# Seven-product pairs of a hybrid decoder layer: three products accumulated on the first one's bank, and a new order of the products

## The chip, the cores and the metric

One Trainium2 chip, one of its cores. The metric is device time in microseconds (us) of one execution, the median of several runs. Engines: PE (TensorE, matmuls) with its weight loads (PEld), DVE (VectorE), ACT (ScalarE), POOL (GpSimd) and SP (SyncE, which issues transfers). PSUM, into which PE writes, has eight banks here, of 128 partitions x 512 fp32 each.

## What is computed

One layer over 1024 tokens of width 1024, in fp32:

```python
h = rms_norm(x, norm_mix_pre[l])
proj = h @ w_in[l]
q, k, v, cb, cc, cx, g_att, g_conv = jnp.split(proj, IN_SPLITS, axis=-1)
...
m   = sigmoid(g_att) * y_att + sigmoid(g_conv) * y_conv
x   = x + RMSNorm_post(m @ W_out)
h   = RMSNorm_pre_ffn(x)
[a, g] = causal_dwconv3(h @ W_up)
x   = x + RMSNorm_post_ffn((gelu(g) * a) @ W_down)
```

y_att is a stick-breaking attention of 8 heads, y_conv a gated short convolution. The change touches the products of h with parts of W_in (the convolution's inputs and the gates) and of h with W_up (1024 x 5632).

## The kernel before

**Numbers and products.** Each fp32 operand of a matmul is held as two fp16 halves, a high and a low one, and a product is three passes (high by high, high by low, low by high) that accumulate in PSUM. Weight tiles of 128 columns are taken two at a time as a pair. A pair's 2 x 2 block product over two halves of the tokens is made with seven block products instead of eight (a Strassen-like scheme): sums and differences of the weight blocks (s_u, ws_u on DVE; their halves wh_u on ACT and DVE) and of the token blocks (hT, hB, tp, tb, n) go in, and the seven results are added up to the pair's two outputs, ca and cg, each with a low (lo) and a high (hi) half of 512 tokens. One product is 12 matmuls of 128 x 512 with start set on the first of those that begin a bank.

The pairs are x0 and x1 (begun in an earlier stage), b0, b1 and g1 to g7 of the mixer (`pair_open`, `pair_prod`), and u0 to u21 of the up-projection (`up_open`, `up_prod`). A pair has three PSUM banks, a, b and c. Before, bank a takes products 1 and 2, one behind the other; bank b takes 6, 7 and 4; bank c takes 5 and 3. Each is a group of its own, so each must be emptied before the next one starts in its bank: 1, 5 and 2 by a copy on ACT (L1413, L1417, L1419 for u), 6, 7, 4 and 3 by an addition on DVE (L1410), and 7 has a second DVE addition of product 5's copy (L1422). PE runs 1, the previous pair's 4, 6, 5, 2, 7, 3. For g pairs the results also go through a sigmoid on ACT.

**Order of the work.** A planner (class Plan) takes all operations with their estimated costs and due times and writes out each engine's instruction list; each engine then runs its list strictly as written and waits on semaphores. Operations marked seq, the products among them, keep the order of the code on PE. Banks come from a ring of eight, five of pool pz (banks 3 to 7) and three of pool pm (banks 0 to 2); a tile gets a bank when its first operation is written out:

```python
self.order, self.n = [p for p, k in pools for _ in range(k)], 0
p = self.order[self.n % len(self.order)]
```

A matmul that starts in a bank waits until the last reader of the tile that had the bank before is done.

**The start of the up-projection.** While the last token tiles are still being normalised and transposed, a few products are run ahead, in this order (pair, product):

```python
PRE = ((0, 1), (1, 1), (0, 2), (1, 2), (2, 1), (2, 2), (0, 5))
```

Names in that stretch: x is the mixer's output with its residual, hn the normalised tile, pt_0 and pt_1 the PSUM tiles with the two halves of tile 7's transposes (L1296), hb their copies (ACT, L1336), tp_0 and tp_1 PSUM tiles with sums of token blocks of tile 6 that DVE makes, n the fp16 halves of those (ACT L1249 the high, DVE L1250 the low), hB and hT the transposed operands that transfers and copies fill from n, hb and tb. jk_u (L66) is a pass over the next weights for their scale, pr_u a tiny matmul for the same purpose, ws_u the weights as they are loaded (SP), wh_u_0 the halves that u2's products 1 and 2 read.

**Later.** Each u pair's ca and cg go through convolution taps (ACT L1434, DVE L1436, twice each), gelu (L1446) and a product (L1447), and the result through the down-projection (pq, pd), with sums kept in DRAM by POOL transfers.

Of the kernel before, what the change touches and what calls it, by code (L numbers as in the profile page):

```python
# [47 lines left out]
class Layer:  # L48
# [693 lines left out]
    def rest(self):  # L742
# [231 lines left out]
        def pair_open(n, p):  # L974
            p.name, p.old = n, begun.get(n)
            p.ca, p.cg = [Buf("x", lambda c=c: self.xp.tile([P, T], F32, tag="x", name=f"{c}{n}")) for c in ("ca", "cg")]
            p.ug = p.ca if p.old else slab(f"ug{n}", [P, T])
            p.bank = {b: Buf("pm", lambda b=b: self.bank(f"p{n}{b}")) for b in ("bc" if p.old else "abc")}
            if p.old:
                p.c = given("s", p.old.c)  # L980
            if n[0] == "g":
                p.sc = Buf("sm", lambda: self.small(f"sc_{n}"))
                V(0.12, lambda: self.mul(p.sc.t[:, 0:1], inv_h, p.sb.t["inv"]), [p.sb], [p.sc])

        def pair_prod(p, i):
            wt, wc = PARTS[i]
            b, ca, cg, ug = p.bank[{1: "a", 2: "a", 5: "c", 3: "c"}.get(i, "b")], p.ca, p.cg, p.ug
            first, gate = i in (1, 6, 5), p.name[0] == "g"

# [12 lines left out]
            p1, pr = ((lambda: p.c.t[:, 0]), (p.c, "0")) if p.old else ((lambda: cg.t[:, lo]), (cg, "l"))  # L1002
            if i == 1:
# [16 lines left out]
            if gate and i in (3, 7, 4):  # L1020
                o, oc, og = {3: (ca, hi, "h"), 7: (cg, hi, "h"), 4: (cg, lo, "l")}[i]
                sigm(o, oc, og, lambda: o.t[:, oc], (o, og))

        def conv_taps(p, i):
# [91 lines left out]
        for n, name in enumerate(PAIRS):  # L1116
            p, kind, i = pw[name], name[0], int(name[1])
            need(n + 2)
            pair_open(name, p)
            start, *middle = (5, 6, 3, 7) if p.old else (1, 6, 5, 2, 7, 3)  # L1120
            pair_prod(p, start)
            if n:
                pair_prod(pw[PAIRS[n - 1]], 4)
                last = PAIRS[n - 1]
                if last[0] == "g":
                    d = int(last[1])
                    sig["gc", d], sig["ga", d] = pw[last].ca, pw[last].cg
                    if d > 1:
                        merge(d)
                else:  # L1130
                    (conv_taps if last[0] == "x" else conv_gate)(pw[last], int(last[1]))
            if name == "g1":
                s_m = p_split()
            for x in middle:
                pair_prod(p, x)
                if name == "x0" and x == 7:
                    wa_branch(6, range(2))
                    wa_branch(7, range(2))
                if name == "g2" and x == 6:
                    wc_branch(0)  # L1140
                    wc_branch(1)
                    merge(0)
                    merge(1)
            if kind == "g":
                if i == 3:
                    wo_sb = wo_sums()
                if i == 5:
                    dn_sums()
                if i == 7:
                    wo = wo_load()  # L1150
                if i == 7:
# [241 lines left out]
        def up_prod(f, i):  # L1393
            p = up[f]
            wt, wc = PARTS[i]
            b = p.bank[{1: "a", 2: "a", 5: "c", 3: "c"}.get(i, "b")]
            ca, cg, ug = p.ca, p.cg, p.ug
            first = i in (1, 6, 5)

            def mm():  # L1400
                n = 0
# [7 lines left out]
            def vadd(o, oc, og, x, xr):  # L1409
                V(C["Vp"], lambda: vec.tensor_tensor(o.t[:, oc], b.t, x.t[:, xr[0]], ALU.add),  # L1410
                  [b, (x, xr[1])], [(o, og)])
            if i == 1:
                A(C["Ah"], lambda: act.activation(cg.t[:, lo], b.t, AF.Copy), [b], [(cg, "l")])  # L1413
            elif i == 6:
                vadd(ca, hi, "h", cg, (lo, "l"))
            elif i == 5:
                A(C["Ah"], lambda: act.activation(ug.t[:, lo], b.t, AF.Copy), [b], [(ug, "l")])  # L1417
            elif i == 2:
                A(C["Ah"], lambda: act.activation(ca.t[:, lo], b.t, AF.Copy), [b], [(ca, "l")])  # L1419
            elif i == 7:  # L1420
                vadd(cg, hi, "h", cg, (lo, "l"))
                V(C["Vh"], lambda: vec.tensor_tensor(cg.t[:, hi], cg.t[:, hi], ug.t[:, lo], ALU.add), [(ug, "l")], [(cg, "h")])  # L1422
# [289 lines left out]
        with tc.manual_schedule(engines={ET.PE, ET.DVE, ET.Activation, ET.SP, ET.Pool}):  # L1712
# [25 lines left out]
            def steps():  # L1738
                for f in range(NFF):
# [228 lines left out]
```

## Time and profile before

| what | value |
|---|---|
| median of 3 runs | 1250.31 us (1249.78 to 1251.18) |
| the profiled execution | 1250.17 us, span of its instructions 1248.5 us |
| mean granted PE clock | 0.998 |
| busy PE / PEld | 1232.6 us (99%) / 559.0 us (45%) |
| busy DVE / ACT / POOL | 1051.7 us (84%) / 841.9 us (67%) / 86.3 us (7%) |

The span runs from the first to the last instruction; 1.67 us of the execution's time lie outside it. Busy PE is counted from modelled ends, so a product of 12 matmuls shows as 2.75 us although the next one starts 2.59 us after it. In rows of the timeline, a square bracket gives the idle time of the engine ahead of the row and who ended it; x12 is the count of instructions in the row.

### The profile page before, as it was taken

What the parts mean: (1) busy time and instruction counts of PE and PEld (TensorE: products, weight loads), DVE (VectorE), ACT (ScalarE), POOL (GpSimd) and SP (SyncE); (2) the same over time, 40 slices, a digit from 0 to 9 for tenths busy, and PEclk for the clock granted to TensorE, in tenths of its full rate; (3) what the DMA queues carried; (4) which work ended last, traced back from release to release, by engine and by line L of the source; (5) the groups of instructions that cost most, each with busy time, mean ns of one, the idle gap of its engine ahead of it and who ended that gap; (6) DMA issues with size and microseconds to landing.
All of it is one profiled execution on the core that took longest, in us unless ns stands there. A gap on an engine that the chain in (4) does not pass through costs nothing.

```text
span 1248.5 us, 16492 instructions
## 1 busy us (share of the span) xinstructions
PE 1232.6 (99%) x6065; PEld 559.0 (45%) x6065; DVE 1051.7 (84%) x1661; ACT 841.9 (67%) x1219; POOL 86.3 (7%) x113
## 2 busy tenths in 40 slices
PE   9999999999999999999999999999999999999997
PEld 4444444444444444444444444444444444444443
DVE  7988889856999776569899999799799879979976
ACT  7766666736758465665676669778777967878424
POOL 1100000000000000001100001002100300211003
PEclk9999999999999999999999999999999999999999
DMA  8755677661214121657853205415921961594608
GB/s 280 158 134 107 141 131 178 146 147 34 69 68 135 35 68 51 220 186 169 218 144 135 68 11 218 177 34 101 261 77 19 193 194 34 99 255 150 170 3 133
DMA packets 148932, 160.81 MB, mean 129 GB/s; under 512 B 114425, under 2 KB 114553, under 8 KB 148850
## 3 DMA queue, kind: packets, MB, share of 16 engines
q1 hardware_dynamic: 138480, 123.05, 35.3%
q0 software_dynamic: 10368, 36.70, 14.2%
q8 instruction: 47, 0.77, 0.2%
q14 instruction: 35, 0.29, 0.1%
q10 hardware_dynamic: 2, 0.00, 0.0%
HBM read 92.88 MB, written 37.75 MB: 105 GB/s over the span
## 4 chain that ended last, share of the span: by engine, by line
PE 45%; DVE 2%; DMA 2%; ACT 1%; issue 1%; POOL 1%; POOLq 0%; DVEq 0%; ACTq 0%
PE pq L1563 12%; PE pd L1633 2%; PE pd L1666 1%; DMA ws_u<-w_up_nt 1%; PE pu7b L1404 1%; PE pu20b L1404 1%; PE pu17b L1404 1%; PE pu15b L1404 1%; PE pu13b L1404 1%; PE pu10b L1404 1%; PE pu9b L1404 1%; PE pu6b L1404 1%; PE pu4b L1404 1%; PE pu2b L1404 1%; PE pu21b L1404 1%
## 5 line engine op out<-in xcount | busy, mean ns | idle before, releaser
L1404 PEld LDWEIGHTS <-wh_u 128*128 128x128 f16 x1848 | 179.2, 98 | 218.6 <-issue 2.0
L992 PEld LDWEIGHTS <-wh_g 128*128 128x128 f16 x588 | 57.1, 98 | 68.6
L827 DVE SCALAR_TENSOR_TENSOR wh_u<-ws_u,sc_u,wh_u 128x1024 f16<-128x1024 f32 (+1 forms) x66 | 72.2, 1103 | 13.9 <-ACT wh_u L825 13.4
L1208 PE MATMUL py<-wo,m 128*128 128x512 f16 x384 | 83.3, 379 | 0.0
L825 ACT ACTIVATE wh_u<-ws_u,sc_u 128x1024 f16<-128x1024 f32 (+1 forms) x66 | 66.4, 1008 | 23.6 <-PE pu0c L1404 4.2
L1567 ACT ACTIVATE st<-pq,sd 128x512 f32<-128x512 f32 x112 | 73.9, 699 | 9.9 <-DVE ua L1447 5.6
L791 POOL DMA_DIRECT2D acc<-st x56 | 43.8, 783 | 426.8 <-ACT st L1567 426.8
L66 ACT ACTIVATE jk_u<-ws_u 128x1024 bf16<-128x1024 f32 x44 | 46.4, 1054 | 23.6 <-DMA ws_u<-w_up_nt 23.2
L624 DVE TENSOR_TENSOR_SCAN e<-e,mask 128x512 f32<-128x512 f32 (+3 forms) x64 | 48.6, 806 | 13.3 <-ACT e L617 13.3
L1208 PEld LDWEIGHTS <-m 128*128 128x128 f16 x384 | 37.4, 98 | 44.9
L1436 DVE SCALAR_TENSOR_TENSOR ua<-ca,cw_a,ua 128x1023 f32<-128x1023 f32 (+1 forms) x44 | 56.2, 1278 | 1.0 <-ACT ua L1434 0.9
L1436 DVE SCALAR_TENSOR_TENSOR ug<-cg,cw_g,ug 128x1023 f32<-128x1023 f32 (+1 forms) x44 | 56.2, 1277 | 0.1
L617 ACT ACTIVATE e<-z,cz 128x1024 f32<-128x1024 f32 (+3 forms) x48 | 42.3, 896 | 20.5 <-PE z L595 14.9
L638 ACT ACTIVATE w<-e 128x1024 f16<-128x1024 f32 (+3 forms) x48 | 38.8, 837 | 12.4 <-DMA wt<-w 7.5
L459 PE MATMUL pcc<-hT,wh_cc 128*128 128x512 f16 x192 | 44.6, 380 | 0.8 <-ACT u L575 0.8
L459 PE MATMUL pk<-hT,wh_k 128*128 128x512 f16 x192 | 43.1, 379 | 0.0
L459 PE MATMUL pq<-hT,wh_q 128*128 128x512 f16 x192 | 43.0, 379 | 0.0
L1563 PE MATMUL pq<-wq,fx 128*128 128x512 f16 x192 | 42.8, 379 | 0.0
L1563 PE MATMUL pq<-wq,fy 128*128 128x512 f16 x192 | 42.7, 379 | 0.0
L924 PE MATMUL pywc<-p,wh_wc 128*128 128x512 f16 x192 | 42.6, 379 | 0.0
L1563 PE MATMUL pq<-wq,fs 128*128 128x512 f16 x192 | 42.1, 379 | 0.0
L624 DVE TENSOR_TENSOR_SCAN e<-e,cr,mask 128x512 f32<-128x512 f32 x32 | 39.8, 1272 | 0.9 <-ACT e L617 0.6
(791 smaller groups left out, 2751.2 us busy)
## 6 DMA issues: line engine op xcount, KB each, us to landing
acc<-st POOLq DMA_DIRECT2D x56, 512.0 KB, 5.9
ws_u<-w_up_nt SPq DMA_DIRECT2D x44, 512.0 KB, 4.0
ds<-w_down SPq DMA_DIRECT2D x18, 512.0 KB, 15.1
wt_g<-w_in_nt SPq DMA_DIRECT2D x14, 512.0 KB, 3.5
x<-x SPq DMA_DIRECT2D x8, 512.0 KB, 8.4
wr_wo<-w_out SPq DMA_DIRECT2D x8, 512.0 KB, 3.6
ws_wo<-w_out SPq DMA_DIRECT2D x8, 512.0 KB, 4.2
xr<-x SPq DMA_DIRECT2D x8, 512.0 KB, 4.5
```

The costliest lines, as they stand in the source:

```text
L66: self.nc.scalar.activation(self.junk(f"jk_{name}"), src, AF.Square, accum_out=acc)
L459: pe.matmul(ps.t, w.t[:, wi, ds(k * P, P)], hT[:, hi, k, ds(c * NH, NH)], start=k == 0 and p == 0, stop=k == KD - 1 and p == 2)
L624: vec.tensor_tensor_scan(x, x, m[:, ::-1], ONE if diag else cr.t[:, h:h + 1], ALU.mult, ALU.max)
L791: j = pl.add(eng, 0.45 if eng == "SP" else 1.14, lambda: e.dma_start(dst(), srcf(), **kw), r, [b] if w is None else w, ahead=AHEAD["load"] ...
L825: A(C["As" if big else "Ash"], lambda: act.activation(dst.t[:, 0, dsl], src.t[:, ssl], AF.Copy, scale=sb.t["s"]), [(src, sreg), sb], [(dst ...
L827: V(C["V" if big else "Vh"], lambda: vec.scalar_tensor_tensor(dst.t[:, 1, dsl], src.t[:, ssl], sb.t["s"], dst.t[:, 0, dsl], ALU.mult, ALU. ...
L992: pe.matmul(b.t, p.w[wt].t[:, wi, ds(wc * NH + k * P, P)], block(i, h, k), start=first and n == 0, stop=n == 3 * KH - 1, skip_group_check= ...
L1208: pe.matmul(b.t, m16[k].t[:, h_, ds(tt * P, P)], wo[k].t[:, w_, sl], start=k == 0 and p == 0, stop=k == 7 and p == 2)
L1404: pe.matmul(b.t, p.w[wt].t[:, wi, ds(wc * NH + k * P, P)], block(i, h, k), start=first and n == 0, stop=n == 3 * KH - 1, skip_group_check= ...
L1436: V(C["V"], lambda lag=lag: vec.scalar_tensor_tensor(u.t[:, lag:], c.t[:, :T - lag], sm.t[:, 2 - lag:3 - lag], u.t[:, lag:], ALU.mult, ALU ...
L1563: pe.matmul(b.t, fa[p].t[:, h, ds(fo * NH + tt * P, P)], wa[p].t[:, x, ds(wo * NH, NH)], start=first and n == 0, stop=n == 5, skip_group_c ...
L1567: A(C["Ah"], lambda tt=tt, b=b, st=st: act.activation(st.t[:, tt % 2, :], b.t, AF.Copy, scale=q.sd.t[:, 0:1]), [b, q.sd], [(st, str(tt % 2 ...
```

## The change

For all pairs but x0 and x1, products 6, 7 and 4 are no longer started afresh but accumulate on product 1 in bank b. So bank b holds product 1 first and is copied by ACT; then 1 + 6, copied by ACT; then 1 + 6 + 7, to which DVE adds the copy of 5; then 1 + 6 + 7 + 4, copied by ACT (in g pairs the sigmoid reads it straight from the bank). Bank a takes product 2 alone, to which DVE adds the copy of 1. Bank c is as before. The DVE additions per pair go from five to three (those of products 2, 7 and 3), the ACT copies from three to four. The order on PE becomes 1, previous 4, 2, 6, 5, 7, 3. The matmuls are as many as before.

```diff
-            b, ca, cg, ug = p.bank[{1: "a", 2: "a", 5: "c", 3: "c"}.get(i, "b")], p.ca, p.cg, p.ug
-            first, gate = i in (1, 6, 5), p.name[0] == "g"
+            ca, cg, ug, gate = p.ca, p.cg, p.ug, p.name[0] == "g"
+            chain = not p.old
+            b = p.bank[({2: "a", 5: "c", 3: "c"} if chain else {1: "a", 2: "a", 5: "c", 3: "c"}).get(i, "b")]
+            first = i in ((1, 2, 5) if chain else (1, 6, 5))
...
-            start, *middle = (5, 6, 3, 7) if p.old else (1, 6, 5, 2, 7, 3)
+            start, *middle = (5, 6, 3, 7) if p.old else (1, 2, 6, 5, 7, 3)
...
         def up_prod(f, i):
...
-            b = p.bank[{1: "a", 2: "a", 5: "c", 3: "c"}.get(i, "b")]
-            ca, cg, ug = p.ca, p.cg, p.ug
-            first = i in (1, 6, 5)
+            b = p.bank[{2: "a", 5: "c", 3: "c"}.get(i, "b")]
+            ca, cg = p.ca, p.cg
+            first = i in (1, 2, 5)
...
+            def copy(o, oc, og):
+                A(C["Ah"], lambda: act.activation(o.t[:, oc], b.t, AF.Copy), [b], [(o, og)])
             if i == 1:
-                A(C["Ah"], lambda: act.activation(cg.t[:, lo], b.t, AF.Copy), [b], [(cg, "l")])
+                copy(cg, lo, "l")
             elif i == 6:
-                vadd(ca, hi, "h", cg, (lo, "l"))
+                copy(ca, hi, "h")
             elif i == 5:
-                A(C["Ah"], lambda: act.activation(ug.t[:, lo], b.t, AF.Copy), [b], [(ug, "l")])
+                copy(cg, hi, "h")
             elif i == 2:
-                A(C["Ah"], lambda: act.activation(ca.t[:, lo], b.t, AF.Copy), [b], [(ca, "l")])
+                vadd(ca, lo, "l", cg, (lo, "l"))
             elif i == 7:
-                vadd(cg, hi, "h", cg, (lo, "l"))
-                V(C["Vh"], lambda: vec.tensor_tensor(cg.t[:, hi], cg.t[:, hi], ug.t[:, lo], ALU.add), [(ug, "l")], [(cg, "h")])
+                vadd(cg, hi, "h", cg, (hi, "h"))
             elif i == 3:
                 vadd(ca, hi, "h", ca, (hi, "h"))
             else:
-                vadd(cg, lo, "l", cg, (lo, "l"))
+                copy(cg, lo, "l")
...
-                    for i in (6, 5, 2, 7, 3):
+                    for i in (2, 6, 5, 7, 3):
```

`pair_prod` for b and g pairs changes in the same way. PRE stays, so u0, u1 and u2 run products 1 and 2 ahead, now in banks b and a.

Where instructions stand follows from the planner. The first place is PE around tile 7's transposes, before and after; the last column names the engine on whose semaphore a row waits. Before:

```order
L1296 MATMUL pt_0_6006<-ident,hn_5883 128x128 [waits DVE_49]
...
L1296 MATMUL pt_1_6017<-ident,hn_5883 128x128 x4
L1404 LDWEIGHTS wh_u_0_5999 [waits Activation_49]
L1404 MATMUL pu2a<-hT,wh_u_0_5999 128x512
...
L813 MATMUL pr_u_6050<-rb_u_6012,ones 128x1 [waits Activation_49]
...
L1404 MATMUL pu2a<-hT,wh_u_0_5999 128x512 [waits Activation_49]
```

After:

```order
L1317 MATMUL pt_0_5993<-ident,hn_5865 128x128 [waits DVE_49]
...
L1317 MATMUL pt_1_6001<-ident,hn_5865 128x128 [waits Activation_49]
...
L1425 MATMUL pu2b<-hT,wh_u_0_5987 128x512 [waits Activation_49]
...
L813 MATMUL pr_u_6032<-rb_u_5990,ones 128x1 [waits DVE_49]
...
L1425 MATMUL pu2a<-hT,wh_u_0_5987 128x512
```

The matmuls stand in the same order; the waits and the banks are others. Before, pt_0 and pt_1 lie in banks 2 and 3, u2's bank a is 6 and pr_u's is 7. After, pt_0, pt_1 and u2's bank b are all bank 3: the second half of the transposes waits for the ACT copy hb of the first, and u2's product 1 for the copy of the second. pr_u's bank is 7, which held tp_0, and its wait is for DVE's third piece of n. u2's second product (bank 1) has no wait of its own.

The second place is ACT in the same stretch (cg, ca: the pair's results; L1434 of the changed kernel is the copy in `up_prod`, L1270 n, L1357 hb, L1350 the copies into hT and hB). Before:

```order
L1413 ACTIVATE cg_5982<-pu1a 128x512
L825 ACTIVATE wh_u_0_5999<-ws_u_0_5742,sc_u_5899 128x1024
L66 ACTIVATE jk_u_1_6001,sm_u_5924<-ws_u_1_5958 128x1024
L1419 ACTIVATE ca_6004<-pu0a 128x512
L1249 ACTIVATE n_6_6015<-tp_0_5904 128x512
L1249 ACTIVATE n_6_6015<-tp_1_5906 128x512
L1336 ACTIVATE hb_6038<-pt_0_6006 128x512
L1336 ACTIVATE hb_6038<-pt_1_6017 128x512
L1419 ACTIVATE ca_6043<-pu1a 128x512
L1329 ACTIVATE hT<-hb_6038 128x4x128
L1329 ACTIVATE hB<-tb_0_6045 128x4x128
L1413 ACTIVATE cg_6054<-pu2a 128x512
```

After:

```order
L1434 ACTIVATE cg_5962<-pu1b 128x512
L66 ACTIVATE jk_u_1_5983,sm_u_5906<-ws_u_1_5939 128x1024
L825 ACTIVATE wh_u_0_5987<-ws_u_0_5724,sc_u_5881 128x1024
L1270 ACTIVATE n_6_5999<-tp_0_5886 128x512
L1270 ACTIVATE n_6_5999<-tp_1_5888 128x512
L1357 ACTIVATE hb_6021<-pt_0_5993 128x512
L1357 ACTIVATE hb_6021<-pt_1_6001 128x512
L1350 ACTIVATE hT<-hb_6021 128x4x128
L1350 ACTIVATE hB<-tb_0_6026 128x4x128
L1434 ACTIVATE cg_6048<-pu2b 128x512
L1350 ACTIVATE hB<-tb_0_6026 128x4x128
L1270 ACTIVATE n_6_5999<-tp_0_5886 128x512
```

jk_u moved ahead of wh_u_0, the two copies of product 2 went to DVE, and n's third piece stands behind the copy of u2's product 1. On DVE, x of tile 7 moved ahead of three scalar operations on pr_u (L808, L810, L811).

The third place is ACT at the end of pair u5, whose bank c is pu5c. Before:

```order
L1434 ACTIVATE ug_6610<-cg_6559,cw_g_6636 128x1024
L1419 ACTIVATE ca_6744<-pu5a 128x512
L1417 ACTIVATE ug_6780<-pu5c 128x512
L1446 ACTIVATE ug_6610<-ug_6610 128x1024
L66 ACTIVATE jk_u_0_6801,sm_u_6800<-ws_u_0_6747 128x1024
```

After (L1467 is the gelu, L1455 the convolution's first term):

```order
L1455 ACTIVATE ug_6716<-cg_6544,cw_g_6526 128x1024
L825 ACTIVATE fy_1_6731<-ua_6528,sp_f_6641 128x1024
L825 ACTIVATE wq_5_6734<-wr_1_6430,sp_dn_5231 128x1024
L66 ACTIVATE jk_u_1_6737,sm_u_6681<-ws_u_1_6624 128x1024
L1434 ACTIVATE ca_6755<-pu5b 128x512
L1467 ACTIVATE ug_6716<-ug_6716 128x1024
L1434 ACTIVATE cg_6687<-pu5c 128x512
L825 ACTIVATE fx_0_6791<-ua_6169,sp_f_6641 128x1024
```

The previous pair's gelu moved from behind the copy of product 5 to ahead of it. It stands so in ten of the u pairs.

More of the change, by code (lines that the diff above doesn't have):

```diff
@@ L976, in pair_open @@
             p.ca, p.cg = [Buf("x", lambda c=c: self.xp.tile([P, T], F32, tag="x", name=f"{c}{n}")) for c in ("ca", "cg")]
[L977 removed]
+            p.ug = p.ca if p.old else p.cg
             p.bank = {b: Buf("pm", lambda b=b: self.bank(f"p{n}{b}")) for b in ("bc" if p.old else "abc")}
@@ L1002, in pair_prod @@
             p1, pr = ((lambda: p.c.t[:, 0]), (p.c, "0")) if p.old else ((lambda: cg.t[:, lo]), (cg, "l"))
-            if i == 1:
+            def copy(o, oc, og):
+                A(C["Ah"], lambda: act.activation(o.t[:, oc], b.t, AF.Copy), [b], [(o, og)])
+            if chain:
+                if i == 1:
+                    copy(cg, lo, "l")
+                elif i == 6:
+                    copy(ca, hi, "h")
+                elif i == 5:
+                    copy(cg, hi, "h")
+                elif i == 2:
+                    vadd(ca, lo, "l", lambda: cg.t[:, lo], (cg, "l"))
+                elif i == 7:
+                    vadd(cg, hi, "h", lambda: cg.t[:, hi], (cg, "h"))
+                elif i == 3:
+                    vadd(ca, hi, "h", lambda: ca.t[:, hi], (ca, "h"))
+                elif gate:
+                    sigm(cg, lo, "l", lambda: b.t, b)
+                else:
+                    copy(cg, lo, "l")
+            elif i == 1:
                 A(C["Ah"], lambda: act.activation(cg.t[:, lo], b.t, AF.Copy), [b], [(cg, "l")])
@@ L1019, in pair_prod @@
                 vadd(cg, lo, "l", p1, pr)
-            if gate and i in (3, 7, 4):
-                o, oc, og = {3: (ca, hi, "h"), 7: (cg, hi, "h"), 4: (cg, lo, "l")}[i]
+            if gate and i in (2, 3, 7):
+                o, oc, og = {2: (ca, lo, "l"), 3: (ca, hi, "h"), 7: (cg, hi, "h")}[i]
                 sigm(o, oc, og, lambda: o.t[:, oc], (o, og))
@@ L1411, in vadd, with copy @@
                   [b, (x, xr[1])], [(o, og)])
+            def copy(o, oc, og):
+                A(C["Ah"], lambda: act.activation(o.t[:, oc], b.t, AF.Copy), [b], [(o, og)])
             if i == 1:
-                A(C["Ah"], lambda: act.activation(cg.t[:, lo], b.t, AF.Copy), [b], [(cg, "l")])
+                copy(cg, lo, "l")
             elif i == 6:
-                vadd(ca, hi, "h", cg, (lo, "l"))
+                copy(ca, hi, "h")
             elif i == 5:
-                A(C["Ah"], lambda: act.activation(ug.t[:, lo], b.t, AF.Copy), [b], [(ug, "l")])
+                copy(cg, hi, "h")
             elif i == 2:
-                A(C["Ah"], lambda: act.activation(ca.t[:, lo], b.t, AF.Copy), [b], [(ca, "l")])
+                vadd(ca, lo, "l", cg, (lo, "l"))
             elif i == 7:
-                vadd(cg, hi, "h", cg, (lo, "l"))
-                V(C["Vh"], lambda: vec.tensor_tensor(cg.t[:, hi], cg.t[:, hi], ug.t[:, lo], ALU.add), [(ug, "l")], [(cg, "h")])
+                vadd(cg, hi, "h", cg, (hi, "h"))
             elif i == 3:
@@ L1425, in up_prod @@
             else:
-                vadd(cg, lo, "l", cg, (lo, "l"))
+                copy(cg, lo, "l")
         def conv(f, u, c, idx, name):
```

## The prediction

> **What bounds the kernel now.** I read the shares of the engines first, then the waits of TensorE (PE), then windows over the stages that the diff touches, then the timeline of the one window in which PE stands. The page and the waits:
>
> ```profile
> PE 1232.6 (99%) x6065; PEld 559.0 (45%) x6065; DVE 1051.7 (84%) x1661; ACT 841.9 (67%) x1219; POOL 86.3 (7%) x113
> PE pu2a L1404 <- ACT cg L1413: 1.7, 1, 1.7
> PE pu0b L1404 <- DVE ca L1410: 1.1, 1, 1.1
> ```
>
> PE is busy for 1232.6 of 1248.5 us; 15.9 us of idle time are all that the whole kernel has. The waits name the tile that waited, who released it, and us in total, times, longest. Two of them lie in products of pairs: u2's second product waited 1.7 us for the ACT copy that empties its bank, and u0's product 7 waited 1.1 us for the DVE addition that empties its bank. Columns of the windows: window, its us, busy us of PE, weight loads, DVE, ACT, POOL, then the granted clock, DMA share and GB/s.
>
> ```profile
> 640.00:650.00 10.00, 8.30 (x44) 4.26 (x43) 8.98 (x17) 8.12 (x16) 0.00 (x0) 1.00 0.46 101
> 650.00:660.00 10.00, 8.94 (x42) 3.92 (x41) 9.68 (x18) 4.52 (x7) 0.00 (x0) 1.00 0.52 125
> 700.00:1100.00 400.00, 400.00 (x1874) 181.56 (x1872) 359.97 (x534) 305.79 (x424) 40.38 (x52) 1.00 0.47 118
> 1241.00:1244.00 3.00, 0.00 (x0) 0.00 (x0) 2.17 (x7) 0.49 (x2) 0.93 (x1) 0.98 0.67 131
> 1244.00:1248.50 4.50, 0.00 (x0) 0.00 (x0) 1.05 (x2) 0.00 (x0) 0.00 (x0) 0.50 0.31 118
> 1236.87 4.07 PE L1666 MATMUL pd<-wdh,f 128*128 128x512 f16 x27
> ```
>
> From 700 to 1100 us PE never stands, while DVE is busy for 90% and ACT for 76% of it. Lighter DVE work earns nothing there. In 640 to 660 PE stands for 1.70 + 1.06 us: that is the largest gain which the change has in reach, 2.8 us or 0.22%. The last three rows serve below (the last is PE's final group of matmuls, from the timeline).
>
> **The steady pairs.** Per pair, two DVE operations go and one ACT copy comes; matmuls stay as many.
>
> ```profile
> L1422 DVE TENSOR_TENSOR cg<-cg,ug 128x512 f32<-128x512 f32 x22 | 15.0, 682 | 0.0
> 662.46 2.75 PE L1404 MATMUL pu1b<-hB,wh_u 128*128 128x512 f16 x12
> 665.05 2.75 PE L1404 MATMUL pu1c<-hB,wh_u 128*128 128x512 f16 x12
> 665.44 0.69 DVE L1410 TENSOR_TENSOR ca<-pu1b,cg 128x512 f32<-128x512 f32 x1
> 667.64 2.75 PE L1404 MATMUL pu1b<-hB,wh_u 128*128 128x512 f16 x12
> 667.85 0.59 ACT L1417 ACTIVATE ug<-pu1c 128x512 f32<-128x512 f32 x1
> 729.88 2.75 PE L1404 MATMUL pu5c<-hB,wh_u 128*128 128x512 f16 x12
> 734.45 1.27 DVE L1436 SCALAR_TENSOR_TENSOR ug<-cg,cw_g,ug 128x1022 f32<-128x1022 f32 x1
> 735.82 0.60 ACT L1417 ACTIVATE ug<-pu5c 128x512 f32<-128x512 f32 x1
> 736.31 1.05 ACT L1446 ACTIVATE ug<-ug 128x1024 f32<-128x1024 f32 x1
> ```
>
> 31 pairs by 2 by 0.68 us are 42 us off DVE; 31 by 0.59 us are 18 us more on ACT. Both are priced at nothing for the end, since PE's 100% windows cover them. What the change adds on PE's path is shorter gaps: in the new order product 7 returns to the bank of product 6 after one other product, and 3 to that of 5 after one. A product is 2.59 us from start to start. The rows of u1 in the kernel before are that same pattern: 6 at 662.46, 5 at 665.05, 7 at 667.64 on the bank of 6. The addition that emptied it ran at 665.44 to 666.13, 1.51 us ahead of need, and PE's starts stay 2.59 apart. The copy of 5 began 0.05 us after its product's end (665.05 + 2.75 = 667.80) and ended 0.64 us after it. A copy must end about 2.4 us after its product (2 by 2.59 - 2.75); against that stands the copy of u5's product 5, which ended at 736.42, 3.8 us after the end at 732.63. There ACT was late because the copy stood behind other work, and two products of gap hid it. In ten of the later pairs the new order puts the gelu, which waits for DVE's convolution taps, directly ahead of this copy. At u5 the second tap ended at 735.72; two additions of 0.68 us less ahead of it on DVE bring that to 734.35, then gelu 1.05 and copy 0.60: 736.0. The bank is needed at 729.88 + 3 by 2.59 = 737.65, so 1.65 us are to spare. Bounds for all steady pairs: 0 to ten by (3.8 - 2.4) = 14 us; I take 0, as the u1 rows are the same pattern and u5's margin is positive.
>
> The Trainium skill, page Perfetto Trace Analysis, section Optimizing Tensor Performance, says that independent matmul groups should rotate through different PSUM banks so that the evacuation of one overlaps the matmuls of the next. By that rule taken strictly, three returns per pair to one bank would each cost an evacuation of about 0.7 us, 31 by 3 by 0.7 = 65 us (E below); by the u1 rows, where one other product in between covers it, the sum has 0. The rule fits better where nothing lies between, and that is the next part.
>
> **The start of the up-projection (640 to 660 us).** Here the sum is made. Columns: start, us, engine, line, operation, tiles.
>
> ```profile
> 633.52 0.69 DVE L832 TENSOR_TENSOR ws_u<-ws_u,ws_u 128x512 f32<-128x512 f32 x1
> 634.45 1.28 DVE L1232 SCALAR_TENSOR_TENSOR x<-hn,r_post,xr 128x1024 f32<-128x1024 f32 x1
> 635.75 0.33 SPq L791 DMA_DIRECT2D ws_u<-w_up_nt  x1
> 637.98 1.15 ACT L825 ACTIVATE wh_u<-ws_u,sc_u 128x1024 f16<-128x1024 f32 x1 [0.52 <-PE pu0a L1404]
> 640.05 1.06 ACT L66 ACTIVATE jk_u<-ws_u 128x1024 bf16<-128x1024 f32 x1 [0.92 <-DMA ws_u<-w_up_nt]
> 640.37 1.04 PE L1296 MATMUL pt<-ident,hn 128*128 128x128 f32 x8
> 641.11 0.58 ACT L1419 ACTIVATE ca<-pu0a 128x512 f32<-128x512 f32 x1
> 641.24 2.75 PE L1404 MATMUL pu2a<-hT,wh_u 128*128 128x512 f16 x12
> 641.58 1.07 ACT L1249 ACTIVATE n<-tp 128x512 f16<-128x512 f32 x2
> 642.54 1.09 ACT L1336 ACTIVATE hb<-pt 128x512 f32<-128x512 f32 x2
> 643.83 0.17 PE L813 MATMUL pr_u<-rb_u,ones 128*128 128x1 bf16 x1
> 644.49 0.67 ACT L1329 ACTIVATE hB<-tb 128x512 f16<-128x512 f32 x1
> 645.01 0.64 ACT L1413 ACTIVATE cg<-pu2a 128x512 f32<-128x512 f32 x1
> 645.70 2.75 PE L1404 MATMUL pu2a<-hT,wh_u 128*128 128x512 f16 x12 [1.70 <-ACT cg L1413]
> 646.01 0.64 ACT L1249 ACTIVATE n<-tp 128x512 f16<-128x512 f32 x1
> 647.26 0.69 DVE L1250 TENSOR_TENSOR n<-tp,n 128x512 f16<-128x512 f32 x1 [0.17 <-DMA hB<-n]
> 648.28 2.75 PE L1404 MATMUL pu0c<-hB,wh_u 128*128 128x512 f16 x12
> 650.87 2.75 PE L1404 MATMUL pu0b<-hB,wh_u 128*128 128x512 f16 x12
> 653.94 0.68 DVE L1410 TENSOR_TENSOR ca<-pu0b,cg 128x512 f32<-128x512 f32 x1
> 654.68 2.76 PE L1404 MATMUL pu0b<-hB,wh_u 128*128 128x512 f16 x12 [1.06 <-DVE ca L1410]
> 650.95 3.09 DMA hT<-n
> ```
>
> Of the seven products written at the head of this stage, four run before tile 7's transposes, and three behind them. With product 2 in a bank of its own, u0 and u1 hold four banks here instead of two, so the tiles behind them get others. In the changed program both halves of tile 7's transposes, pt_0 and pt_1, and then u2's first product all lie in bank 3; pr_u, which PE runs between u2's two products, gets the bank of tp_0, the sums of tile 6, which DVE reads last in n's third piece. PE works in order, so each of these is a wait for everything behind it. Step by step, with the durations above:
>
> 1. The weights' DMA at 635.75 waits for x (634.45 + 1.28 = 635.73), and in the new order DVE does x right after the row at 633.52 and not behind three scalar operations: 0.3 us earlier. So jk_u starts at 640.05 - 0.3 = 639.75; it stands ahead of wh_u now (before: behind it). The next ACT row came 1.06 us after jk_u's start: wh_u at 640.8, and with 1.15 us n at 641.95. From n's start to hb's start were 0.96 us: hb's first half at 642.9, some 0.6 us long (two took 1.09): 643.5.
> 2. pt_0 is done at about 640.9, as before. pt_1 needs its bank emptied by that first half: starts at 643.55, takes half of 1.04: 644.1. The second half of hb: 644.7. u2's first product starts at 644.75, where before it started at 641.24: 3.5 us later.
> 3. Its start-to-start 2.59 us give 647.34, its modelled end 647.5. The ACT copy of it (0.05 and 0.60 as for u1's product 5) starts at 647.55. Behind it on ACT stand a copy to hB and n's third piece, each 0.52 us after the one ahead (644.49 to 645.01): n at 648.6, ends 649.2; DVE's part of n 0.69: 649.95. Only then may pr_u run, and with it u2's second product: 650.05, against 645.70 before. The 1.70 us wait is gone, and 2.6 us stand in its place.
> 4. u0's products 5 and 6 follow without a gap (before, too): 652.65 and 655.25, against 648.28 and 650.87, 4.4 us late. Product 7 goes to the bank of 6 with nothing between: end at 658.0, ACT copy 0.65, start 658.7, against 654.68. Before, the addition at 653.94 had stood behind a weight operation on DVE and PE had waited 1.06 us; now 0.8. That returns 0.3 us.
> 5. After this PE is covered again: products follow without a gap at 4.0 us later than before. The transposed tiles come in time: n's third piece at 649.95 and two transfers of 3.1 us with n's last pieces between (two of 0.64 on ACT, one of 0.69 on DVE: 2 us) give 658.2, and the product that needs them starts at 661.3.
>
> Sum: idle time added 2.6 (pt_1) + 0.7 (u2's product 1) + 2.6 (pr_u), idle time taken away 1.7 (u2) + 0.3 (u0) = +3.9 to +4.0 us, and nothing for the steady pairs. The profiled execution took 1250.17 us, 0.14 us under the median of 1250.31, so 1254.2 us, or +0.3%. Bounds of the start of the up-projection: from below, if ACT is never late (rival A), +2.0 us; below that, if the banks were free in time, -2.8 us; from above, +4.0 and one product at half clock (rival C), +6.6 us.
>
> **The rivals.** A, no measurable change: the 2.6 us wait of pt_1 rests on jk_u waiting for its weights (0.92 us of idle before it at 640.05) at the head of ACT's queue. If that transfer lands 1.9 us earlier, hb's first half follows pt_0 directly at 640.95, u2's first product starts at 642.85, and the loss is 4.0 - 1.9 = 2.1 us: 1252.3 us. From 1.5 us earlier on, it is under 2.5 us, the bound of what can be told. For it: transfers vary; against it: the row before took 4.2 us from issue to use, and the issue moves by 0.3 us alone. Chance 0.17, with the smaller cases in which only one of the two new stalls appears.
>
> B, faster: the two waits of 1.7 and 1.1 us go and no other comes: 1250.2 - 2.8 = 1247.4 us. It needs hb's copies and n's third piece to be done when PE reaches them, so ACT some 4 us ahead of the sums above. The two rows of waits speak for it, ACT's full row of work from 640.05 to 645.0 against it. Chance 0.05.
>
> C, the clock: after PE's last matmul (1236.87 + 4.07 = 1240.94) the granted clock is 0.98 over 1241 to 1244 and 0.50 after, so it fell some 3 us into the idle time. In the forecast PE does 0.5 us of transposes in the 3.85 us from 640.9 to 644.75. If the clock falls there, u2's first product takes twice as long: 2.6 us more, 1256.8 us. Against it: the wait of 1.70 us left the clock at 1.00, and the single idle stretches (2.6 us) are shorter than 3 us. Chance 0.13. The Trainium skill, page TensorE: Matmul & The Clock Gate, section What's actually happening, has the clock halve after an idle window of about 3.4 us that runs freely; by it one such window could be met or missed here, while the rows alone put the limit near 3 us.
>
> D, steady stalls: the copy of 5 behind the gelu is late by 0.5 us in each of the ten pairs: 1254.2 + 5 = 1259 us. It decides as soon as that copy ends over 2.4 us after its product. For it the copy at 735.82, against it the margin of 1.65 us. Chance 0.10.
>
> E, every return to a bank waits for its evacuation although another product lies between: the 65 us above, 1319 us. Against it the starts of u1's products, 2.59 us apart. Chance 0.01.
>
> **How the numbers follow.** Forecast 0.53, A 0.17, B 0.05, C 0.13, D 0.10, E 0.01, and 0.01 for no effect at all. A measurement of this kernel tells 0.2% (2.5 us) from no change. Faster: B, 0.05. Same: A and no effect, 0.18. Slower: forecast, C, D and E, 0.77. The range takes in the forecast, C at its upper end and A down to a loss of 1.5 us, and leaves out B, no effect, D and E: 1251.7 to 1256.8 us.
>
> **What would show it.** Right: PE waits at pt, pu2b and pr_u between 640 and 650 for hb (twice) and n, together about 5.9 us, and none of 1.7 us on pu2; u0's product 7 waiting about 0.8 us for an ACT copy; PE at 100% from 660 on; DVE busy some 42 us less and ACT 18 us more. Wrong: a wait of pu..c in the gelu pairs (D), a granted clock under 1.00 near 645 (C), the transfer of u2's weights landing before 638 (A), or pt without a wait (B).

## The result, and the profile after

The changed kernel takes 1257.43 us (median of six runs, 1255.81 to 1258.49); the kernel before took 1251.11 us beside it (six runs, 1249.78 to 1252.58). The ratio is 1.005 with a 95% interval of 1.0037 to 1.0063: 6.3 us slower, where +3.9 us was forecast. The sign was right and the size was not; the time lies 0.6 us above the upper end of the range given. The kernel before was 0.8 us slower in this set than the 1250.31 us to which the forecast was added, so the difference, 6.3 against 3.9, says more than the time alone.

The profiled execution of the changed kernel took 1258.49 us (span 1256.8), the slowest of its six, so it shows somewhat more loss than the median. Of its page the shares of the engines:

```profile
PE 1237.9 (98%) x6065; PEld 560.6 (45%) x6065; DVE 1014.5 (81%) x1599; ACT 857.0 (68%) x1250; POOL 86.1 (7%) x113
```

and of PE's waits those of the up-projection:

```profile
PE pt L1317 <- ACT hb L1357: 2.6, 1, 2.6
PE pr_u L813 <- DVE n L1271: 2.5, 1, 2.5
PE pu0b L1425 <- ACT ca L1434: 0.7, 1, 0.7
PE pu2b L1425 <- ACT hb L1357: 0.7, 1, 0.7
```

DVE is 37 us less busy and ACT 15 us more (42 and 18 were forecast), and it earns nothing. The waits at the start of the up-projection are the forecast ones, tile by tile. But PE is also busy for 5.3 us more with as many matmuls. Idle time does not make PE busier: something made the matmuls longer. The windows (same columns as before, the granted clock third from the end) say what:

```profile
640.00:650.00 10.00, 6.68 (x23) 3.07 (x22) 5.99 (x11) 5.39 (x9) 0.00 (x0) 0.68 0.36 86
650.00:660.00 10.00, 7.47 (x28) 2.89 (x27) 5.00 (x9) 3.23 (x6) 0.00 (x0) 0.80 0.27 53
700.00:1100.00 400.00, 400.00 (x1875) 181.48 (x1874) 343.23 (x501) 312.91 (x436) 37.69 (x49) 1.00 0.44 115
643.50:643.75 0.25, 0.00 (x0) 0.00 (x0) 0.25 (x2) 0.25 (x1) 0.00 (x0) 0.83 0.00 0
650.25:650.50 0.25, 0.25 (x2) 0.15 (x1) 0.00 (x0) 0.00 (x0) 0.00 (x0) 0.52 0.00 0
653.75:654.00 0.25, 0.25 (x2) 0.10 (x1) 0.10 (x1) 0.00 (x0) 0.00 (x0) 0.81 1.07 215
657.25:657.50 0.25, 0.25 (x2) 0.10 (x1) 0.25 (x2) 0.25 (x2) 0.00 (x0) 0.87 0.00 0
```

The clock was at 1.00 through both of these 10 us windows before; now its means are 0.68 and 0.80. The quarter-microsecond rows lie on its four edges (0.83 is 66% of the slice at 1.00 and the rest at 0.50): it fell at 643.67, came back at 650.49, fell at 653.91 and came back at 657.32. The timeline of PE shows what ran in these two spells:

```profile
640.61 0.60 PE L1317 MATMUL pt<-ident,hn 128*128 128x128 f32 x4
643.85 1.11 PE L1317 MATMUL pt<-ident,hn 128*128 128x128 f32 x4 [2.64 <-ACT hb L1357]
645.65 5.13 PE L1425 MATMUL pu2b<-hT,wh_u 128*128 128x512 f16 x12 [0.68 <-ACT hb L1357]
653.30 0.16 PE L813 MATMUL pr_u<-rb_u,ones 128*128 128x1 bf16 x1 [2.53 <-DVE n L1271]
653.33 4.44 PE L1425 MATMUL pu2a<-hT,wh_u 128*128 128x512 f16 x12
657.60 2.75 PE L1425 MATMUL pu0c<-hB,wh_u 128*128 128x512 f16 x12
663.63 2.75 PE L1425 MATMUL pu0b<-hB,wh_u 128*128 128x512 f16 x12 [0.68 <-ACT ca L1434]
1245.81 4.07 PE L1687 MATMUL pd<-wdh,f 128*128 128x512 f16 x27
```

Both of u2's products ran at half clock for most of their time: the first shows 5.13 us instead of 2.75, the second starts 4.27 us ahead of its successor instead of 2.59. With the second half of the transposes (1.11 us, against 0.66 at full clock in a run below) that is 2.4 + 1.7 + 0.45 = 4.5 us. From the start of pt_0 to u0's product 5 the kernel before took 648.28 - 640.37 = 7.91 us and this one takes 657.60 - 640.61 = 16.99 us. Of the 9.1 us, 2.64 + 0.68 + 2.53 - 1.70 = 4.15 are waits, 4.5 the clock, and some 0.4 the run-out of the last matmul where PE stops (2.75 us against 2.59 for a product that nothing follows): it stops three times here, and once before. pt_0 itself started 0.24 us later, and at u0's product 7 the wait is 0.38 us shorter, so there the lag is 663.63 - 654.68 = 8.95 us. PE's last group is 1245.81 - 1236.87 = 8.94 us late: nothing was lost or made good over the 580 us between them. Behind PE's last matmul 0.6 us came back: the span ends 6.92 us after it, where before it ended 7.52 us after it.

### The profile page after: what moved, and what is told of

Its sections match the earlier page's. It is cut to its first block, busy times and chain, and to the rows that moved or that the text cites. A ratio compares the mean times of both kernels' runs of the same rounds, so it can differ in the third digit from the quotient of the medians.

```text
span 1256.8 us, 16464 instructions
## 1 busy us (share of the span) xinstructions
PE 1237.9 (98%) x6065; PEld 560.6 (45%) x6065; DVE 1014.5 (81%) x1599; ACT 857.0 (68%) x1250; POOL 86.1 (7%) x113
## 4 chain that ended last, share of the span: by engine, by line
PE 45%; DVE 2%; ACT 1%; issue 1%; DMA 1%; POOL 1%; POOLq 0%; DVEq 0%; ACTq 0%
PE pq L1584 12%; PE pd L1654 2%; PE pu2b L1425 1%; PE pu20b L1425 1%; PE pu19b L1425 1%; PE pu8b L1425 1%; PE pu6b L1425 1%; PE pu16b L1425 1%; PE pu12b L1425 1%; PE pu4b L1425 1%; PE pu3b L1425 1%; PE pu21b L1425 1%; PE pu13b L1425 1%; PE pu10b L1425 1%; PE pu18b L1425 1%
```

## The experiments

The theory after the result: (1) the steady pairs are neutral; (2) the loss is made where pt_0, pt_1 and u2's first product share bank 3 and pr_u waits for bank 7; (3) the idle time there also lowers the clock, which costs as much again. The rivals: the steady pairs lose after all and the start is less; or the clock is a coincidence. Diffs are against the changed kernel and are shortened: a condition stands in place of the constant that the runs use, and what else goes with it is told in words.

**The old scheme for u0, u1 and u2 alone** (banks, copies, additions and order of before for these three pairs, the rest as changed).

```diff
         def up_prod(f, i):
+            chain = f > 2
```

> The first three up-projection pairs (u0, u1, u2) go back to the old scheme, so the head of the up-projection gets the old banks; all mixer pairs and u3 to u21 keep the new scheme. Theory 1 (the whole loss of 6 us lies in 640 to 664 us: PE waits for banks, and the clock falls in the idle time): within 1.5 us of before, PE waits of 1.7 and 1.1 us at u2 and u0 are back, clock 1.00 there. Theory 2 (part of the loss comes from shorter gaps in the steady pairs): 2 us or more over before, with PE waits at products of the pairs from u3 on.

Measured 1250.12 us, ratio 0.9998 (0.9988 to 1.0007). PE's waits in it are those of the kernel before, and its window from 700 to 1100 us is as full:

```profile
PE pu2a L1433 <- ACT cg L1442: 1.5, 1, 1.5
PE pu0b L1433 <- DVE ca L1439: 1.4, 1, 1.4
```

```profile
700.00:1100.00 400.00, 400.00 (x1874) 181.55 (x1872) 346.69 (x506) 315.95 (x442) 40.25 (x52) 1.00 0.46 119
```

So the new scheme in 28 of the 31 pairs costs nothing and brings nothing that can be measured (-1.5 to +0.9 us): the loss hangs on u0, u1 and u2.

**The new scheme for u0, u1 and u2 alone** (the other u pairs and the b and g pairs as before).

```diff
         def up_prod(f, i):
+            chain = f < 3
```

> The reverse: only u0, u1 and u2 use the new scheme, all other pairs the old one. Theory 1: the whole loss is here, 1255.5 to 1258.5 us, with the waits at the transposes of tile 7, at u2's first product and at pr_u (2.6, 0.7, 2.5 us) and a granted clock of 0.5 in two stretches. Theory 2: under 1254 us.

Measured 1262.3 us, ratio 1.009 (1.0075 to 1.0106). Its waits, and u2's two products in its timeline:

```profile
PE pr_u L816 <- DVE n L1275: 2.5, 1, 2.5
PE pt L1324 <- ACT hb L1364: 2.5, 1, 2.5
PE pu21b L1433 <- DVE cg L1439: 2.1, 1, 2.1
PE pu21b L1433 <- DVE ca L1439: 0.8, 1, 0.8
```

```profile
645.03 4.42 PE L1433 MATMUL pu2b<-hT,wh_u 128*128 128x512 f16 x12 [0.69 <-ACT hb L1364]
652.00 4.35 PE L1433 MATMUL pu2a<-hT,wh_u 128*128 128x512 f16 x12
```

The three waits and the two slow products are there with three pairs alone. The time is above what was expected: 2.1 + 0.8 us of waits stand at u21, the last pair, where the mixture made the planner write DVE's list in another order, and the product behind the first of them, a wait of 2.14 us in the timeline, takes 4.31 us, again at half clock (from 1187.74 to 1191.15). Neither pure kernel waits at u21, so this run confirms the place but not the size.

**Filling the first idle stretch.** The first half of tile 7's transposes is done six times over, so PE works where it stood. First with the planner told of the longer work:

```diff
-                    for k in range(KH):
+                    for k in list(range(KH)) * (6 if tt == 7 and e == 0 else 1):
...
-                pl.add("PE", 0.45, turn(e), [h], [pt[e]])
+                pl.add("PE", 0.45 * (6 if tt == 7 and e == 0 else 1), turn(e), [h], [pt[e]])
```

> The changed kernel, but the first half of tile 7's transposes is done six times over (the same result), so PE has 2.2 us more work where it stood for 2.6 us. The banks and their waits are as in the changed kernel. Theory 1 (the clock fell because PE was idle): the clock stays at 1.00 through u2's first product, which takes 2.75 us and not 5.1; 2.5 us or more are won against the changed kernel, 1253.5 to 1256 us; the later wait at pr_u can still cost one stretch of half clock. Rival (the clock falls for another reason, or transposes do not count as work): 1257 to 1258 us, u2's first product at 5 us.

Measured 1252.98 us, ratio 1.0019 (1.0008 to 1.003), half a microsecond below the range expected, and the clock stayed at 1.00. But the planner, told that PE is late, put wh_u ahead of jk_u and n's third piece ahead of the copy of u2's first product on ACT, and pr_u's wait went as well: two things were changed. So again without the cost:

```diff
-                    for k in range(KH):
+                    for k in list(range(KH)) * (6 if tt == 7 and e == 0 else 1):
```

> As the fill above (first half of tile 7's transposes six times over), but the planner is told the old cost, so ACT's list and the wait of pr_u on n stay as in the changed kernel: only PE's idle time of 2.6 us is filled. Theory 1 (idle time lowers the clock): u2's first product at 2.75 us instead of 5.1, the waits at u2's first product (0.7) and pr_u (2.5) stay; the bank waits alone then cost 4.0 to 4.3 us over before (1254.2 to 1254.5), and up to 1.7 us more where the 2.5 us wait lowers the clock for one stretch. Rival (the earlier fill was faster only because pr_u's wait had gone, and the clock is not the filled idle time's doing): u2's first product at 4 to 5 us, 1256 us or more.

Measured 1254.65 us, ratio 1.0037 (1.0024 to 1.0051), with ACT's order and the waits of the changed kernel. u2's products in its timeline:

```profile
644.16 2.75 PE L1433 MATMUL pu2b<-hT,wh_u 128*128 128x512 f16 x12 [0.69 <-ACT hb L1364]
649.47 4.32 PE L1433 MATMUL pu2a<-hT,wh_u 128*128 128x512 f16 x12
```

Twenty more transposes on PE, and the loss against the kernel before fell from 6.3 to 4.5 us. u2's first product is back at 2.75 us; the second, behind the 2.53 us of idle time that were not filled, is not.

**Filling both stretches, or the second alone.** Behind u2's first product ten more matmuls go into u0's bank a, whose contents have been read; the planner is not told, and every wait, bank and list of ACT and DVE stays. Once with the transposes six times as in the last run, once with them as they were.

```diff
+                if (f, i) == (2, 1):
+                    for n in range(10):
+                        pe.matmul(up[0].bank["a"].t, p.w[wt].t[:, 0, ds(wc * NH, P)], block(i, 0, 0), start=n == 0, stop=n == 9, skip_group_check=True)
```

> The changed kernel with both idle stretches of PE filled and every wait, bank and ACT order kept: the first half of tile 7's transposes six times as in the run before, and behind u2's first product ten more matmuls of 128 x 512 into u0's bank a, whose contents have been read (10 by 0.216 = 2.16 us, inside the 2.53 us in which PE would wait for pr_u's bank). Theory (bank waits and the clock add up): the granted clock stays at 1.00, both products of u2 take 2.75 us, pr_u still runs when DVE has done n's third piece, and against the 1254.65 us with the first stretch alone filled the second product's half clock goes (4.32 against 2.75, 1.6 us): 1253.0 us, range 1252.4 to 1253.9. That is then the price of the waits alone, to be held against the forecast's 1254.2. Rival (the second product is slow for another reason, for instance DMA or reads of the same operand): it stays near 4.3 us and the time at 1254.7.

> The same with the second stretch alone filled (ten more matmuls behind u2's first product, transposes once). Theory: the clock still falls in the first idle stretch, u2's first product takes 4.4 to 5.1 us and the filling matmuls run at half clock in part; the second product then depends on the window in which the clock comes back: with PE busy from product 1 on, it comes back within 3.4 to 6.8 us and the second product takes about 2.75. Time 1255.0 to 1256.5, between the 1253.0 of both filled and the 1257.4 of none. Rival (idle time is not what lowers the clock): as slow as the changed kernel, 1257.4 or more.

Both filled: 1254.88 us, ratio 1.0039 (1.0025 to 1.0052). The second alone: 1255.98 us, ratio 1.0048 (1.0035 to 1.006). The timeline with both filled:

```profile
639.48 2.78 PE L1324 MATMUL pt<-ident,hn 128*128 128x128 f32 x24
644.29 2.75 PE L1433 MATMUL pu2b<-hT,wh_u 128*128 128x512 f16 x12 [0.69 <-ACT hb L1364]
649.60 2.75 PE L1433 MATMUL pu2a<-hT,wh_u 128*128 128x512 f16 x12
652.18 2.75 PE L1433 MATMUL pu0c<-hB,wh_u 128*128 128x512 f16 x12
658.21 2.75 PE L1433 MATMUL pu0b<-hB,wh_u 128*128 128x512 f16 x12 [0.69 <-ACT ca L1446]
```

and with the second alone:

```profile
645.44 3.64 PE L1433 MATMUL pu2b<-hT,wh_u 128*128 128x512 f16 x12 [0.68 <-ACT hb L1364]
651.64 2.75 PE L1433 MATMUL pu2a<-hT,wh_u 128*128 128x512 f16 x12
```

Each filled stretch restores the product behind it and no other, so the clock falls because PE stands. (With the second alone filled the first product is still slow, though at 3.64 us less so than the 4.4 to 5.1 expected.) The run with both filled came out 1 us above its expectation at the median (its profiled execution, at 1253.1, was inside it), and against the changed kernel, timed in another set beside a kernel before that was 1 us slower, the saving could be 2.6 us or 1.4. So both were run again on one chip:

> The changed kernel itself, beside the kernel with both idle stretches filled, on one chip: their difference is the price of the half clock at the median, free of the difference of about 1 us between the kernel before in one set of runs and in another. If the clock is a term of its own, about as large as the waits' run-to-run part: 1256.0 to 1258.0 us, 1.4 to 3 us above the kernel with both filled. If the waits are the whole loss at the median and the clock falls only in some runs: equal to the filled one within 0.7 us, near 1255.

> The kernel with both idle stretches filled (transposes six times, ten more matmuls behind u2's first product), beside the changed kernel. Theory: the clock at 1.00 throughout and 1253.5 to 1255.3 us, the price of the waits alone, 1.4 to 3 us below the changed kernel. Rival (the clock costs nothing at the median): no difference to the changed kernel over 0.7 us.

The changed kernel took 1256.47 us, ratio 1.0052 (1.0039 to 1.0065), and with both stretches filled 1253.4 us, ratio 1.0026 (1.0015 to 1.0036); the kernel before 1250.1 us. The clock is worth 3.1 us of a loss of 6.4 (some 1 to 5 us, by the spread of these runs), and the waits 3.3 us (1.9 to 4.5; in the earlier set 4.9, 3.1 to 6.5). The traces give the split more closely. From the start of pt_0 to that of u0's product 7 the kernel before takes 654.68 - 640.37 = 14.31 us, and the kernel with both stretches filled 658.21 - 639.48 = 18.73 us, in both of its traces: 4.4 us for the waits with the run-outs. In this second trace of the changed kernel the waits are the same within 0.2 us, but the two spells lie otherwise:

```profile
642.80 0.66 PE L1317 MATMUL pt<-ident,hn 128*128 128x128 f32 x4 [2.79 <-ACT hb L1357]
644.14 4.03 PE L1425 MATMUL pu2b<-hT,wh_u 128*128 128x512 f16 x12 [0.68 <-ACT hb L1357]
650.72 4.15 PE L1425 MATMUL pu2a<-hT,wh_u 128*128 128x512 f16 x12
654.71 2.75 PE L1425 MATMUL pu0c<-hB,wh_u 128*128 128x512 f16 x12
```

Here the clock's part is 4.03 - 2.75 and 654.71 - 650.72 - 2.59, together 2.7 us, where the first trace had 4.5: that execution took 1255.66 us, the first one 1258.49. So between these two traces of one kernel the waits stay and the cost of the clock varies.

**Another bank for pt_1**, from pool pm; the bank rotation then gives u2's first product bank 2 and pr_u bank 1.

```diff
+                    if tt == 7 and e == 1:
+                        while self.pz.order[self.pz.n % 8] is not self.pm3:
+                            self.pz.n += 1
```

> The changed kernel, but the second half of tile 7's transposes takes a bank of the other pool (bank 1), after which u2's first product gets bank 2, pr_u bank 1 and u2's second product bank 3, and u0's product 5 the bank that holds tp_0. Theory 1: no wait of pt on hb and none of pr_u on n; what is left is a wait of u2's first product for its weights (about 1.5 us) and of u0's product 5 for n; no fall of the clock; 1249.5 to 1251.5 us, equal to before within 0.1%. Rival (the loss is the new order of ACT's queue, with jk_u ahead of the weights, whatever the banks): 1253 us or more.

Measured 1252.12 us, ratio 1.0016 (1.0007 to 1.0026). Of its waits, and a window with the clock:

```profile
PE pu0c L1433 <- DVE n L1275: 1.6, 1, 1.6
PE pu2b L1433 <- ACT wh_u L828: 1.4, 1, 1.4
PE pu2b L1433 <- DVE wh_u L830: 0.7, 1, 0.7
```

```profile
640.00:650.00 10.00, 6.44 (x34) 2.94 (x32) 7.02 (x13) 8.29 (x14) 0.00 (x0) 1.00 0.51 77
```

The other bank for pt_1, and those that follow from it, bring the loss from 6.3 to 1.9 us (1252.12 against 1250.2), 0.6 us above the range expected. What is left goes with the order on ACT, with jk_u ahead of wh_u: u2's first product waits 2.1 us for its weights, and u0's product 5 1.6 us for n. The next run puts that order back.

**The bank and the order**: pt_1's bank as above, and the planner told the six-fold cost of the transposes without their being repeated, which puts wh_u back ahead of jk_u on ACT, and n's third piece ahead of the copy of u2's first product. Then the same with PRE's last entry changed, so that a product lies between u0's 6 and 7.

```diff
-                pl.add("PE", 0.45, turn(e), [h], [pt[e]])
+                pl.add("PE", 0.45 * (6 if tt == 7 and e == 0 else 1), turn(e), [h], [pt[e]])
...
-PRE = ((0, 1), (1, 1), (0, 2), (1, 2), (2, 1), (2, 2), (0, 5))
+PRE = ((0, 1), (1, 1), (0, 2), (1, 2), (2, 1), (2, 2), (0, 6))
```

> As the bank experiment (tile 7's second half in bank 1), and the planner is told a six times higher cost for the first half of the transposes, which are run once: its list for ACT then has the weights wh_u ahead of jk_u again and n's third piece ahead of the copy of u2's first product. Theory (the 1.9 us left with the banks mended are ACT's order): no wait of u2's first product, u0's product 5 at 647.5 or earlier after PE's start of the stage as before, one wait of 0.7 at u0's product 7: 1 us under before, 1248.5 to 1250 us. Rival (new scheme costs elsewhere): 1251.5 us or more.

> As the one before, and u0's product 6 runs ahead of its product 5, so that product 5 lies between 6 and 7 and no product returns to its bank at once. Theory: the 0.7 us wait at u0's product 7 goes too, 1.7 us under before (1248 to 1249.5 us). Rival (the tiles that 6 and 7 read are late, the waits move to the transposed tiles): equal to the run before it.

Measured 1250.42 us, ratio 1.0005 (0.9996 to 1.0014), and 1250.2 us, ratio 0.9996 (0.9987 to 1.0005). The loss is gone within the noise (-0.5 to +1.8 and -1.6 to +0.6 us), but neither beats the kernel before: they came out 0.4 and 0.7 us above the ranges expected. Of the waits that the swap removes, a part returns at the product that now comes first. With (0, 5):

```profile
PE pu0c L1433 <- DVE n L1275: 1.2, 1, 1.2
PE pu0b L1433 <- ACT ca L1442: 0.7, 1, 0.7
```

and with (0, 6):

```profile
PE pu0b L1433 <- ACT hB L1357: 0.9, 1, 0.9
PE pu0b L1433 <- DVE hB L1358: 0.4, 1, 0.4
```

**The old scheme for u0 and u1 alone**, with the same entry of PRE changed and nothing else.

```diff
         def up_prod(f, i):
+            chain = f > 1
```

> u0 and u1 keep the old scheme (one bank for products 1 and 2), u2 and all later pairs and the mixer pairs have the new one, and u0's product 6 runs ahead of 5. No bank is short at tile 7. Theory: the waits of 1.7 and 1.1 us of before are gone, a wait of some 2 us of u2's first product for its weights (behind jk_u on ACT) takes their place: 1249 to 1250.5 us. Rival (steady stalls of the new scheme): 1251.5 us or more.

Measured 1249.97 us, ratio 0.9999 (0.999 to 1.0008), as expected in time. The waits lie otherwise in its trace: u2's first product waits 0.35 + 0.72 us for its weights, and not some 2 us, and u0's product 6 waits 2.17 us for n. Its runs reach from 1248.77 to 1253.32 us, and the profiled one, at 1253.15, has the clock in it, as its timeline and two slices show:

```profile
646.51 2.75 PE L1433 MATMUL pu2a<-hT,wh_u 128*128 128x512 f16 x12
651.42 4.44 PE L1433 MATMUL pu0b<-hB,wh_u 128*128 128x512 f16 x12 [2.17 <-DVE n L1275]
```

```profile
651.75:652.00 0.25, 0.25 (x3) 0.14 (x1) 0.25 (x2) 0.00 (x0) 0.00 (x0) 0.70 0.00 0
655.25:655.50 0.25, 0.25 (x3) 0.12 (x2) 0.00 (x0) 0.00 (x0) 0.00 (x0) 0.97 0.77 160
```

A single wait of 2.17 us was followed by a half-clock spell from 651.85 to 655.26, and the product in it started 4.28 us ahead of its successor.

## Why the prediction was wrong in size

- **The steady pairs at nothing: right.** The run with the old scheme for three pairs is at 0.9998, and PE is at 400.00 of 400 us from 700 to 1100 before and after. Rivals D and E are out. The margin that D turned on, at u5, from the timeline after (the gelu runs just ahead of the copy):

```profile
744.19 0.60 ACT L1434 ACTIVATE cg<-pu5c 128x512 f32<-128x512 f32 x1
746.58 2.75 PE L1425 MATMUL pu5c<-hT,wh_u 128*128 128x512 f16 x12
```

  The copy ended at 744.79, 1.79 us ahead of the next product in its bank (1.65 were forecast).

- **Steps 1 to 4, the waits: right.** pt_1 2.64 us (2.6 forecast), u2's first product 0.68 (0.7), pr_u 2.53 (2.6), none of 1.7 at u2, and 0.68 at u0's product 7 (0.8, or 0.7 by step 4's own figures). jk_u came as forecast at the head of ACT's queue, and n's third piece behind the copy of u2's first product:

```profile
640.16 1.06 ACT L66 ACTIVATE jk_u<-ws_u 128x1024 bf16<-128x1024 f32 x1 [2.38 <-DMA ws_u<-w_up_nt]
643.20 0.59 ACT L1357 ACTIVATE hb<-pt 128x512 f32<-128x512 f32 x1
650.81 0.60 ACT L1434 ACTIVATE cg<-pu2b 128x512 f32<-128x512 f32 x1 [4.03 <-PE pu2b L1425]
651.82 0.59 ACT L1270 ACTIVATE n<-tp 128x512 f16<-128x512 f32 x1
```

  Rivals A and B are out with these rows: jk_u still waited 2.38 us for its weights, and hb's first half started 2 us after pt_0 was done. With the clock held up the waits cost 3.3 and 4.9 us in two sets (1.9 to 4.5 and 3.1 to 6.5), and the forecast's +3.9 lies in both. From pt_0 to u0's product 7 the filled kernel's traces have 4.4 us, where step 4 had 4.0.

- **The time of u2's two products in steps 3 and 4, and so the sum: here it failed.** Step 3 gives the first product 2.59 us from start to start, and step 4 the second (650.05 to 652.65); the first showed 5.13 us and the second started 4.27 us ahead of its successor. Rival C was the case that happened, and it was given 0.13 on two wrong grounds. First, it was held that single idle stretches under 3 us leave the clock alone: 2.64 us, and in other runs 2.17 and 2.14 us, were followed by half clock. The bound of 3 us had been read off the end of the kernel, where PE does nothing for seven microseconds; that row can tell how late the clock fell there, not how little idle time is enough. Nor is the 3 us a constant: over the fourteen traces the clock fell between 2.2 and 5.1 us after PE's last matmul. Second, C was priced at one product, but there were two long waits, and each had a product behind it: up to 4.5 us where C had 2.6. The term that is missing from the sum measures 3.1 us at the median; with it the sum would have been 7.0 us, against 6.3 and 6.4 measured. The upper bound, 1256.8 us, lies inside the changed kernel's own runs instead of above them.

- **The busy time of DVE and ACT: mis-sized, without weight in the sum.** 62 DVE operations fewer took 37 us off, 0.60 us each, and 31 ACT copies more added 15 us, 0.49 each. The 0.68 and 0.59 us of the rows overlap with the next operation's where one follows at once, as the starts in the timeline show (658.36 and 658.96 for two DVE rows of 0.68 before).

## What the runs showed of the clock

In the profiled execution after, the edges, 643.67, 650.49, 653.91 and 657.32, are 6.82, 3.42 and 3.41 us apart, so on a grid of about 3.41 us that the idle stretches do not start. The fall behind PE's last matmul, at 1254.65, lies 179 such slots after 643.67, and in each of the other traces too all edges fit one grid, so its slots can be told wherever it has an edge.

The grid slot ahead of the first fall (640.25 to 643.67) has PE busy for 0.96 us, that ahead of the second (650.49 to 653.91) for 0.29 + 0.60 us, that ahead of the fall in the last run told above (648.44 to 651.85) for 0.82 + 0.43 us. Over all slots of the fourteen traces from 14 us on, some 360 in each, the clock, where it stood at 1.00, fell behind every slot in which PE was busy for 1.40 us or less by its modelled ends, and behind none with 1.71 us or more; no slot lies between. The 1.70 us of idle time before the change fell into one slot (643.15 to 646.57, busy for 1.72 us) and had no effect; in the run with pt_1 in another bank the emptiest slots of the stage were busy for 1.95 and 2.14 us. So it is the idle share of a slot that counts, with the limit between 50% and 59% idle in these traces, and what a stretch of some 2 to 3 us costs depends on where the slots fall. The way back is longer: a slot at half clock with PE busy for 2.54 us (643.67 to 647.08) was followed by another, and those with 2.73 us or more by full clock. That is why the first spell took two slots and the second one.

The two traces of the changed kernel, 4.5 and 2.7 us of clock at 1258.49 and 1255.66 us, fit that.

The Trainium skill, page TensorE: Matmul & The Clock Gate, section What's actually happening, gives a free-running window of 3413 ns: the edges agree. Its later rule, no idle gaps over some 3.4 us (section HAM oscillation — how this bites in real kernels), is too wide for these runs, where 2.14 and 2.17 us were enough.

## What to carry over

Where the most loaded engine works in order, look at which tile had a bank before and who reads it last: a scheme that holds two banks more in one stage put three waits for the readers of other tiles on PE, while 37 us less work on DVE was worth nothing beside a PE at 100%. Price a new idle stretch of two microseconds or more on PE twice, once as itself and once as the work behind it at half clock, and count the stretches. A quick test for the second part is to give PE useless work in the gap: the kernel got 3.1 us faster by doing more.
